# SwiGLU's gate and up products with the weights stationary instead of the activations

## The chip, the cores and the metric

The kernel runs on one core of one Trainium2 chip. The metric is device time of that core in microseconds (us). The kernel before took 2026.13 us, the median of three runs (2023.01, 2026.13, 2027.49).

## What is computed

Two stacks of two layers each over 256 tokens of width 1024, all in float32:

```
first stack, twice:   x = x + 0.5 * swiglu(rms_norm(x, g0))
                      x = x + mixer(rms_norm(x))         # two attentions in layer 0, latent attention in layer 1
                      x = x + memory_attention(rms_norm(x), rms_norm(mem))
                      x = x + 0.5 * swiglu(rms_norm(x, g1))
second stack, twice:  x = layer_norm(alpha * x + mixer2(x))
                      x = layer_norm(alpha * x + swiglu(x))
swiglu(h) = (silu(h @ w_gate) * (h @ w_up)) @ w_down     # 1024 -> 2816 -> 1024
rms_norm(x, gain) = x * rsqrt(mean(x * x) + 1e-6) * gain
```

There are six SwiGLUs, each with three weights of 2,883,584 numbers.

## The kernel before

**Dense products.** The 256 tokens are cut into two halves of 128. Float32 operands are split into two parts of type float32r, hi and lo, and a product is the sum in PSUM of three: lo x hi, hi x lo, hi x hi. Weights come in tiles of 512 KB (128 partitions x 1024 numbers): `weights` (L137 to L151) loads one by a DMA on SyncE's queue into one of four kept `wr` slots (L132), ScalarE writes its hi part `wh` (L149, three kept slots), VectorE the lo part `wl` (L150, two kept slots).

**`dense` (L187 to L211)** has the activations stationary: for each half and each block of 128 rows of the weight it issues

```
nc.tensor.matmul(o, xl, wh[:, k], start=first, stop=False)    # L207
nc.tensor.matmul(o, xh, wl[:, k], start=False, stop=False)    # L208
nc.tensor.matmul(o, xh, wh[:, k], start=False, stop=last)     # L209
```

where `xh`, `xl` are 128 features x 128 tokens (tiles `op`, `ol`), and up to 512 columns of the weight move past them. The result has tokens on the partitions. One PSUM bank per half takes it. The last tiles can be held apart (`apart`), in the scope's own `wh` and `wl` slots, to be used for half 0 first.

**`swiglu` (L290 to L311)** takes 512 of the 2816 features at a time (five blocks, and one of 256): the gate product, ScalarE's SiLU straight from PSUM with the norm's r as scale (L303), the up product, VectorE's multiplication of both (L306), and `split_T` (L214 to L225): TensorE transposes the four blocks of each half (L221), ScalarE writes their hi part (L224), VectorE the lo part (L225). Then the down product runs over all 22 blocks, 512 result columns at a time, in 11 tiles each; for the second 512 columns the last four tiles are held apart.

**Around it.** `norm_T` (L261 to L286) makes the transposed operand of the normed x: blocks 0 to 3 of both halves, then blocks 4 to 7. Its rms factor r per token is left to who takes the products (`xT.r`). `ffn1` (L313 to L322) adds half the result to x. `ffn2` (L985) has no norm in front; behind it `post` and `ln` (L943 to L983) do the layer norm, half by half. `dense_T` (L991 to L1013), used in `mixer2`, has the weights stationary and both halves' 256 tokens moving; its matmuls go through `Chain` (L416 to L428; the matmul is L423), which keeps the products into one bank in program order.

**Order of the work and place of the tiles.** Each engine runs its own queue in order; the compiler's scheduler sets the order by program order, with what `later` moves and dependencies. The slots of a phase are given in `SCOPES` by tag; sizes by tag are in `SIZES`: `s` and `ls` slots have 16 float32 columns (64 bytes per partition), all others 128 columns or multiples. A phase's pools lie one behind the other in SBUF in the order of that table, after the kept tiles.

Of the kernel before, what the change touches and what calls it, by code (L numbers as in the profile page):

```python
"""Two stacks of two layers on one core: diff / stick-breaking / latent / memory attention and
SwiGLU with pre-norm, then gated linear attention, RWKV-7 and sparse attention with post-norm.

Dense products: the operands are split exactly into two float32r parts (12 and 11 significant bits)
and three products of parts are summed in PSUM, which keeps float32's accuracy. Tokens are cut into
two halves of 128; the halves' chains are independent but for keys and values."""
# [22 lines left out]
class Core:  # L29
    """Pools, the splitting of float32 operands and the dense products."""  # L30

    # columns of a tile by tag
    SIZES = (("s", 16), ("b05", 128), ("b1", 256), ("b2", 512), ("b4", 1024), ("b8", 2048))
    # slots by phase and tag: in SBUF and in PSUM
    KEEP = dict(x=2, g1=4, v1=1, wr=4, wh=3, wl=2)
    SCOPES = {
        "ffn": (dict(s=10, ls=14, g4=2, b2=6, op=8, ol=8, wh=4, wl=4),
                dict(t=2, d=6)),
        "ffn2": (dict(s=10, ls=8, b2=8, op=8, ol=8, wh=4, wl=4, g2=4),
# [27 lines left out]
    @contextmanager  # L67
    def scope(self, name):
        """Pools of a phase."""
        self.n += 1  # L70
        self.caps = self.SCOPES[name]
        self.count = {}
        self.turn = -1
        with ExitStack() as st:
            pool = lambda t, **k: st.enter_context(self.tc.tile_pool(name=f"{name}_{t}_{self.n}", bufs=1, reuse_waits="tile", **k))
            self.sb = {t: pool(t) for t in self.caps[0] if t != "chains"}
            self.ps = {t: pool(t + "p", space=PSUM) for t, n in self.caps[1].items() if not isinstance(n, str)}
            yield
# [35 lines left out]
    def evac(self, out, in_, scale=None):  # L114
        """PSUM to SBUF, by ScalarE and VectorE in turn."""
# [9 lines left out]
    def raw_weights(self, parts, k0, nk):  # L125
        """Rows k0 : k0 + nk * 128 of parts [(w, first column, columns)] side by side, as [128, nk, columns]."""
# [8 lines left out]

    def weights(self, parts, k0, nk, room=None):
        """The same as (hi, lo), in the kept tiles or in those of the tags in room: one for each, or one for both."""  # L137
        nc = self.nc
        raw = self.raw_weights(parts, k0, nk)
        n = raw.shape[2]  # L140
# [28 lines left out]
    def on(self, stream):  # L169
        """Slots of its own for what the block traces."""  # L170
# [4 lines left out]
    def chain(self):  # L175
        """One of the streams C0, C1, ... in turn: their work overlaps."""
# [4 lines left out]
    def later(self, n):  # L181
        """What the block traces is issued as if traced n instructions later."""
# [4 lines left out]
    def dense(self, lhs, w, n0, nw, done, order=None, apart=()):  # L187
        """Token-major product of 512 columns at most: lhs(h, k) gives the (hi, lo) of the kth block of
        128 rows of the transposed operand of half h; done(h, psum) takes the result. The last tiles of the
        weights, held as apart says one by one, are all used for the first half before the second."""  # L190
# [23 lines left out]
    def split_T(self, src, nb, put):  # L214
        """src [128 tokens, nb blocks of 128] to the (hi, lo) views put(b, m)."""
# [12 lines left out]
    def rstd(self, ss, n, mean_scale, eps, r=None):  # L228
        """(ss * mean_scale + eps) ** -0.5 of [128, n]."""
# [7 lines left out]
    def row_gain(self, ap, n):  # L237
        """A vector on every partition."""
# [5 lines left out]
    def operand(self, nb, groups=None):  # L244
        """Room for nb transposed blocks of both halves, in groups of four or [(tag, blocks)]: put(h, b, m) gives
        the (hi, lo) views [128, m, 128] of blocks b : b + m (within a group), get(h, k) the (hi, lo) of one."""
# [6 lines left out]
        get.both = lambda k: [v[at[k][0]][:, at[k][1]] for v in V]  # L253
        return put, get

    def twin(self):
        """Two long-lived tiles of 256 columns."""
# [3 lines left out]
    def norm_T(self, xs, gain, gates=True):  # L261
        """The transposed and split halves, a function (h, k) -> (hi, lo). With a gain: of the product by it,
        and r[h], what the rms norm multiplies the rows of half h by, is left to who takes the products."""
# [5 lines left out]
        for i in range(2):  # L269
            # the first half may run ahead of the product that still works on the second  # L270
# [19 lines left out]
    def swiglu(self, xT, wg, wu, wd, done):  # L290
        """done(h, n0, psum): columns n0 : n0 + 512 of half h."""
        nc = self.nc
        F = wg.shape[1]
        r = getattr(xT, "r", (1.0, 1.0))
        put, get = self.operand(F // 128)

        for n0 in range(0, F, 512):
            nw = min(512, F - n0)
            g = {}

            def gate(h, ps):
                g[h] = self.t(512)
                nc.scalar.activation(g[h][:, :nw], ps, AF.Silu, scale=r[h])  # L303

            def up(h, ps):
                nc.vector.scalar_tensor_tensor(g[h][:, :nw], ps, r[h], g[h][:, :nw], op0=OP.mult, op1=OP.mult)  # L306
                self.split_T(g[h], nw // 128, lambda b, m: put(h, n0 // 128 + b, m))

            self.dense(xT, wg, n0, nw, gate)
            self.dense(xT, wu, n0, nw, up)  # L310
# [3 lines left out]
    def ffn1(self, layer, j):  # L314
        nc, I = self.nc, self.I
        gain = self.row_gain(I["ffn_norm"][layer, j], 1024)
        xT = self.norm_T(self.x, gain)

        def done(h, n0, ps):
            x = self.x[h][:, n0:n0 + 512]  # L320
            nc.vector.scalar_tensor_tensor(x, ps, 0.5, x, op0=OP.mult, op1=OP.add)

        self.swiglu(xT, I["ffn_w_gate"][layer, j], I["ffn_w_up"][layer, j], I["ffn_w_down"][layer, j], done)

# [1 line left out]
    def load_consts(self, cp):  # L326
        """The constants that the first phase needs."""
# [4 lines left out]
        self.mhalf = self.c["mhalf"]  # L332

    def load_masks(self, cp, cb):
        """The others."""
# [20 lines left out]
def const_pack():  # L356
    """Constants that depend on shapes alone: those in float32, and masks that bfloat16 holds exactly."""
# [4 lines left out]
    # -1 where the row's key is not before the column's, and everywhere  # L362
# [12 lines left out]
    # even tokens, then odd ones  # L375
# [9 lines left out]
    b["causal"] = np.where(c > p, -1e30, 0.0)       # queries on partitions  # L385
    b["strict"] = np.where(p >= c, -1e30, 0.0)      # keys on partitions
    b["keep64"] = np.broadcast_to(np.arange(256)[None] % 64 != 0, (128, 256))
    # within chunks of 64 rows
# [22 lines left out]
# of them: those that the first phase needs  # L411
# [4 lines left out]
class Chain:  # L416
    """Products into one PSUM bank, kept in this order on the tensor engine."""
# [13 lines left out]
class Mix1(Core):  # L431
# [10 lines left out]
    def head_rstd(self, src, nh, d, eps=1e-6, times=1.0, r=None):  # L442
        """times / rms over the d columns of each head of [128, nh * d] (a view [128, nh, d])."""
# [8 lines left out]
    def to_T(self, src, nb, out, w=128, scale=None):  # L452
        """src [128 tokens, nb * w] to out (view [w, nb, 128], or several of rows [(rows, view)])."""
# [18 lines left out]
    def rope_into(self, out, x, nh, d, cos, sin):  # L472
        """out = rotated x, both views [128, nh, d]; cos [128, d] and sin [128, d] carry the gains."""
# [10 lines left out]
    def rope_gain(self, room, cs, sn, gain, d, scale=1.0):  # L484
        """Tables of [128, d] with a gain [128, d] folded in."""
# [1348 lines left out]
```

## Time and profile before

| | |
|---|---|
| median of three runs | 2026.13 us |
| span of the profiled execution | 2021.1 us |
| mean granted clock of TensorE in it | 0.992 |
| busy: TensorE, weight loads, VectorE, ScalarE, GpSimd | 97%, 80%, 60%, 49%, 9% |
| DMA: bytes moved, mean rate | 318.76 MB, 158 GB/s |

The profile is of one execution. Its page gives the span, from the first instruction to the last, and no other time of that execution; 5.0 us separate it from the median of the runs. Times in the rows count from the start of the span. PE is TensorE's matmuls, PEld its weight loads, DVE VectorE, ACT ScalarE, POOL GpSimd, SP SyncE. Matmuls overlap, so the duration of one is longer than the distance between two starts.

### The profile page before, as it was taken

How to read it: one execution, taken by the hardware profiler on the slowest of the kernel's cores; microseconds unless marked ns; L12 is line 12 of the kernel's file. 1: busy time of each engine (PE TensorE's matmuls, PEld its weight loads, DVE VectorE, ACT ScalarE, POOL GpSimd, SP SyncE). 2: the span in 40 equal slices, each digit the busy share in tenths (PEclk: the TensorE clock that was granted, in tenths of full speed). 3: DMA queues.
4: the chain of work that ended last, by engine and by line, in shares of the span. 5: the costliest groups of instructions: out<-in, count | busy, mean ns of one | idle time of the engine just before them, and what ended most of it. 6: DMA issues, size and time to landing. Idle time of an engine off the chain costs nothing.

```text
span 2021.1 us, 28782 instructions
## 1 busy us (share of the span) xinstructions
PE 1951.2 (97%) x10916; PEld 1613.1 (80%) x10916; DVE 1220.9 (60%) x1849; ACT 990.4 (49%) x1549; POOL 191.2 (9%) x269
## 2 busy tenths in 40 slices
PE   8999999899999999898999999999999999999998
PEld 6888778788878888677888888777888787777886
DVE  5555765655555557766655567666555667565555
ACT  5444556554444446655544445543444455434442
POOL 0000401000000001330000012310000213210000
PEclk9999999999999999999999999999999999999999
DMA  7666543466556656234566654314666644026654
GB/s 226 188 194 223 152 136 106 125 198 186 184 179 188 185 193 210 89 100 146 167 187 179 210 148 125 106 43 144 180 180 184 180 140 155 2 84 188 185 179 136
DMA packets 198556, 318.76 MB, mean 158 GB/s; under 512 B 28944, under 2 KB 61969, under 8 KB 198417
## 3 DMA queue, kind: packets, MB, share of 16 engines
q1 hardware_dynamic: 197824, 315.79, 52.2%
q8 instruction: 86, 1.41, 0.3%
q0 software_dynamic: 160, 0.52, 0.1%
q10 hardware_dynamic: 432, 0.60, 0.1%
q14 instruction: 54, 0.43, 0.1%
HBM read 315.82 MB, written 1.05 MB: 157 GB/s over the span
## 4 chain that ended last, share of the span: by engine, by line
PE 53%; DVE 3%; ACT 1%; issue 1%; DMA 1%; POOL 0%; SPq 0%; DVEq 0%; ACTq 0%; POOLq 0%
PE pd L207 12%; PE pd L208 12%; PE pd L209 12%; PE pd L423 4%; PE po L423 2%; PE ppC L423 1%; DVE wl L150 1%; PE pt L221 1%; PE pg L1190 1%; PE pg L423 1%; PE pt L459 0%; PE pq L1466 0%; PE pq L1475 0%; PE pq L700 0%; DMA wr<-in_w_in_dram 0%
## 5 line engine op out<-in xcount | busy, mean ns | idle before, releaser
L150 DVE TENSOR_TENSOR wl<-wr,wh 128x1024 fp32r<-128x1024 f32 (+2 forms) x557 | 677.7, 1219 | 517.0 <-PE pd L208 391.6
L149 ACT ACTIVATE wh<-wr 128x1024 fp32r<-128x1024 f32 (+2 forms) x557 | 585.0, 1051 | 604.0 <-PE pd L209 511.3
L208 PE MATMUL pd<-wl,op 128*128 128x512 f32 (+4 forms) x2136 | 810.1, 380 | 3.9 <-DVE wl L150 3.8
L209 PE MATMUL pd<-wh,op 128*128 128x512 f32 (+4 forms) x2136 | 805.2, 378 | 0.0
L207 PE MATMUL pd<-wh,ol 128*128 128x512 f32 (+4 forms) x2136 | 749.5, 380 | 8.3 <-DVE ol L225 6.9
L207 PEld LDWEIGHTS pd<-wh,ol 128*128 128x128 f32 x2136 | 401.3, 189 | 83.5 <-DVE ol L225 8.4
L208 PEld LDWEIGHTS pd<-wl,op 128*128 128x128 f32 x2136 | 403.6, 189 | 79.4 <-DVE wl L150 7.3
L209 PEld LDWEIGHTS pd<-wh,op 128*128 128x128 f32 x2136 | 403.8, 189 | 71.7
L224 ACT ACTIVATE op<-pt 128x512 fp32r<-128x512 f32 (+1 forms) x118 | 65.8, 564 | 82.6 <-PE pt L221 82.6
L225 DVE TENSOR_TENSOR ol<-pt,op 128x512 fp32r<-128x512 f32 (+1 forms) x118 | 77.0, 656 | 31.7 <-ACT op L224 31.2
L234 POOL TENSOR_TENSOR ls<-s,cf 128x1 f32<-128x1 f32 (+2 forms) x30 | 25.5, 851 | 743.7 <-DVE s L233 563.4
L221 PE MATMUL pt<-cf,b 128*128 128x128 f32 x404 | 63.4, 279 | 11.3 <-DVE b L276 7.9
L221 PEld LDWEIGHTS pt<-cf,b 128*128 128x128 f32 x404 | 50.8, 143 | 24.2 <-DVE b L276 8.3
L423 PE MATMUL pd<-op,wl 128*128 128x256 f32 x208 | 58.5, 281 | 6.3 <-DVE lb2R L1266 4.8
L234 POOL TENSOR_TENSOR s<-s,cf 128x1 f32<-128x1 f32 (+2 forms) x22 | 22.7, 1032 | 442.4 <-DVE s L233 441.1
L423 PE MATMUL pd<-ol,wh 128*128 128x256 f32 x208 | 58.1, 279 | 0.0
L423 PE MATMUL pd<-op,wh 128*128 128x256 f32 x208 | 57.8, 278 | 0.0
L423 PEld LDWEIGHTS pd<-op,wl 128*128 128x128 f32 x208 | 39.1, 188 | 7.5 <-DVE lb2R L1266 5.4
L306 DVE SCALAR_TENSOR_TENSOR b<-pd,ls,b 128x512 f32<-128x512 f32 (+1 forms) x48 | 33.8, 703 | 12.6 <-PE pd L209 12.6
L303 ACT ACTIVATE b<-pd,ls 128x512 f32<-128x512 f32 (+1 forms) x48 | 31.3, 654 | 20.2 <-PE pd L209 20.1
L423 PEld LDWEIGHTS pd<-ol,wh 128*128 128x128 f32 x208 | 39.1, 188 | 0.8 <-issue 0.7
L423 PEld LDWEIGHTS pd<-op,wh 128*128 128x128 f32 x208 | 39.1, 188 | 0.7 <-issue 0.7
(496 smaller groups left out, 1981.2 us busy)
## 6 DMA issues: line engine op xcount, KB each, us to landing
wr<-in_ffn_w_gate_dram SPq DMA_DIRECT2D x132, 512.0 KB, 3.7
wr<-in_ffn_w_up_dram SPq DMA_DIRECT2D x132, 512.0 KB, 3.7
wr<-in_ffn_w_down_dram SPq DMA_DIRECT2D x132, 512.0 KB, 3.7
wr<-in_w_in_dram SPq DMA_DIRECT2D x45, 512.0 KB, 4.6
wr<-in_ab_w_in_dram SPq DMA_DIRECT2D x24, 512.0 KB, 4.2
wr<-in_xm_w_kv_dram SPq DMA_DIRECT2D x16, 512.0 KB, 3.7
wr<-in_w_out_dram SPq DMA_DIRECT2D x16, 512.0 KB, 4.2
wr<-in_ab_w_out_dram SPq DMA_DIRECT2D x8, 512.0 KB, 3.6
```

The costliest lines, as they stand in the source:

```text
L149: nc.scalar.activation(hi, raw, AF.Copy)
L150: nc.vector.tensor_tensor(lo, raw, hi.bitcast(F32), op=OP.subtract)
L207: nc.tensor.matmul(o, xl, wh[:, k], start=first, stop=False)
L208: nc.tensor.matmul(o, xh, wl[:, k], start=False, stop=False)
L209: nc.tensor.matmul(o, xh, wh[:, k], start=False, stop=last)
L221: nc.tensor.transpose(pt[:, i * 128:(i + 1) * 128], src[:, (b0 + i) * 128:(b0 + i + 1) * 128], self.ident)
L224: nc.scalar.activation(hi, v, AF.Copy)
L225: nc.vector.tensor_tensor(lo, v, hi.bitcast(F32), op=OP.subtract)
L234: self.pow = nc.gpsimd.tensor_tensor(r, a, self.mhalf[:, :n], op=OP.pow)
L303: nc.scalar.activation(g[h][:, :nw], ps, AF.Silu, scale=r[h])
L306: nc.vector.scalar_tensor_tensor(g[h][:, :nw], ps, r[h], g[h][:, :nw], op0=OP.mult, op1=OP.mult)
L423: i = self.k.nc.tensor.matmul(out, lhsT, rhs, start=start, stop=stop, skip_group_check=skip)
```

## The change

The gate and up weights are repacked on the host into one array, `ffn_gu` (and `ffn_gu_2`): 11 groups of 256 features, four quarters of the 1024 rows each, and for a group and quarter one contiguous piece of 128 x 1024 numbers that holds, for two blocks of 128 rows, 128 gate columns, 128 up columns, 128 gate columns, 128 up columns. `packed` loads such a piece by one DMA; the splitting (`parted`) stays as it was.

`swiglu` walks over groups. A group has two PSUM banks, each with 256 columns (all tokens) of a gate block and 256 of an up block, and per tile 4 x 2 x 3 matmuls in which 128 x 128 of the weight is stationary and the 256 tokens of both halves move. The result has features on the partitions, as the down product wants its operand, so `split_T` isn't called. Since r now lies along the row, `along` builds a matrix R with r of each token on all partitions, by two plain float32 matmuls (ones x diagonal of r) behind the first group's products; VectorE multiplies the gate by R ahead of SiLU. The up product's r is applied to the result of the down product, as 0.5 r. In `ffn2` there is no r, and SiLU reads PSUM. The down product's code is unchanged. `SCOPES` gets the slots for this.

```diff
-        "ffn": (dict(s=10, ls=14, g4=2, b2=6, op=8, ol=8, wh=4, wl=4),
+        "ffn": (dict(s=10, ls=16, g4=2, b2=6, b1=6, b05=2, lb1=1, op=8, ol=8, wh=4, wl=4),
                 dict(t=2, d=6)),
-        "ffn2": (dict(s=10, ls=8, b2=8, op=8, ol=8, wh=4, wl=4, g2=4),
+        "ffn2": (dict(s=10, ls=8, b2=6, b1=6, op=8, ol=8, wh=4, wl=4, g2=4),
                 dict(t=3, d=5)),
...
+    def packed(self, w, nk):
+        raw = self.kept("wr", 1024)
+        self.nc.sync.dma_start(raw, w)
+        return self.parted(raw.rearrange("p (k n) -> p k n", k=nk))
...
+        get.blocks = lambda b, m: [v[at[b][0]][:, at[b][1]:at[b][1] + m] for v in V]
...
-    def swiglu(self, xT, wg, wu, wd, done):
-        nc = self.nc
-        F = wg.shape[1]
-        r = getattr(xT, "r", (1.0, 1.0))
-        put, get = self.operand(F // 128)
-        for n0 in range(0, F, 512):
-            nw = min(512, F - n0)
-            g = {}
-            def gate(h, ps):
-                g[h] = self.t(512)
-                nc.scalar.activation(g[h][:, :nw], ps, AF.Silu, scale=r[h])
-            def up(h, ps):
-                nc.vector.scalar_tensor_tensor(g[h][:, :nw], ps, r[h], g[h][:, :nw], op0=OP.mult, op1=OP.mult)
-                self.split_T(g[h], nw // 128, lambda b, m: put(h, n0 // 128 + b, m))
-            self.dense(xT, wg, n0, nw, gate)
-            self.dense(xT, wu, n0, nw, up)
+    def along(self, r):
+        nc = self.nc
+        pt, R = self.p("t"), self.l(256)
+        for h in range(2):
+            d = self.t(128)
+            nc.vector.tensor_scalar(d, self.ident, r[h], None, op0=OP.mult)
+            nc.tensor.matmul(pt[:, h * 128:(h + 1) * 128], self.ones, d, start=True, stop=True)
+        nc.scalar.activation(R, pt[:, :256], AF.Copy)
+        return R
+
+    def swiglu(self, xT, wgu, wd, done):
+        nc = self.nc
+        G = wgu.shape[0]
+        put, get = self.operand(2 * G)
+        R = None
+        for g in range(G):
+            banks = [self.p("d") for _ in range(2)]
+            chains = [Chain(self) for _ in banks]
+            for q in range(4):
+                wh, wl = self.packed(wgu[g, q], 2)
+                for i in range(4):
+                    o = banks[i // 2][:, (i % 2) * 256:(i % 2) * 256 + 256]
+                    ch = chains[i // 2]
+                    c = slice(i * 128, i * 128 + 128)
+                    for k in range(2):
+                        xh, xl = xT.both(2 * q + k)
+                        first, last = q == 0 and k == 0, q == 3 and k == 1
+                        ch(o, wl[:, k, c], xh, start=first and i % 2 == 0, stop=False, skip=True)
+                        ch(o, wh[:, k, c], xl, start=False, stop=False, skip=True)
+                        ch(o, wh[:, k, c], xh, start=False, stop=last, skip=True)
+            if R is None and hasattr(xT, "r"):
+                R = self.along(xT.r)
+            y = self.t(512)
+            for b, ps in enumerate(banks):
+                s = self.t(256)
+                if R is None:
+                    nc.scalar.activation(s, ps[:, :256], AF.Silu)
+                else:
+                    nc.vector.tensor_tensor(s, ps[:, :256], R, op=OP.mult)
+                    nc.scalar.activation(s, s, AF.Silu)
+                nc.vector.tensor_tensor(y[:, b * 256:b * 256 + 256], ps[:, 256:], s, op=OP.mult)
+            yv = y.rearrange("p (b t) -> p b t", b=2)
+            hi, lo = get.blocks(2 * g, 2)
+            nc.scalar.activation(hi, yv, AF.Copy)
+            nc.vector.tensor_tensor(lo, yv, hi.bitcast(F32), op=OP.subtract)
         for n0 in range(0, 1024, 512):
             self.dense(get, wd, n0, 512, lambda h, ps: done(h, n0, ps), apart=[("wh", "wl")] * 4 if n0 else ())
...
+        half = [self.l(1) for _ in range(2)]
+        for h in range(2):
+            nc.vector.tensor_scalar(half[h], xT.r[h], 0.5, None, op0=OP.mult)
         def done(h, n0, ps):
             x = self.x[h][:, n0:n0 + 512]
-            nc.vector.scalar_tensor_tensor(x, ps, 0.5, x, op0=OP.mult, op1=OP.add)
+            nc.vector.scalar_tensor_tensor(x, ps, half[h], x, op0=OP.mult, op1=OP.add)
...
+        self.ones = self.consts.tile([128, 128], F32, name="ones")
+        self.nc.gpsimd.memset(self.ones, 1.0)
```

## Rows read from the trace of the kernel before

**Rows 1.** The page, busy us, share of the span, instructions by engine.
```profile
PE 1951.2 (97%) x10916; PEld 1613.1 (80%) x10916; DVE 1220.9 (60%) x1849; ACT 990.4 (49%) x1549; POOL 191.2 (9%) x269
```
**Rows 2.** The page, chain that ended last, share of the span by line.
```profile
PE pd L207 12%; PE pd L208 12%; PE pd L209 12%; PE pd L423 4%; PE po L423 2%; PE ppC L423 1%; DVE wl L150 1%; PE pt L221 1%; PE pg L1190 1%; PE pg L423 1%; PE pt L459 0%; PE pq L1466 0%; PE pq L1475 0%; PE pq L700 0%; DMA wr<-in_w_in_dram 0%
```
**Rows 3.** Windows: us; busy PE, PEld, DVE, ACT, POOL; clock, DMA, GB/s.
```profile
404.10:529.75 125.65, 125.65 (x624) 106.00 (x622) 70.67 (x73) 61.42 (x72) 1.12 (x2) 1.00 0.64 189
529.75:590.89 61.14, 61.14 (x278) 50.45 (x276) 33.36 (x34) 28.00 (x33) 0.55 (x1) 1.00 0.64 206
...
1396.67:1521.36 124.69, 124.69 (x604) 103.59 (x605) 67.20 (x66) 58.32 (x67) 0.00 (x0) 1.00 0.61 178
```
**Rows 4.** Timeline of PE, `ffn1`, 512 columns: start, duration, line, tiles, shape, count.
```profile
110.43 0.63 PE L207 MATMUL pd<-wh,ol 128*128 128x512 f32 x2
...
126.57 0.39 PE L209 MATMUL pd<-wh,op 128*128 128x512 f32 x1
```
**Rows 5.** Timeline of PE, `ffn1`, the last block of 256 columns.
```profile
131.61 0.28 PE L209 MATMUL pd<-wh,op 128*128 128x256 f32 x1
...
139.05 0.28 PE L209 MATMUL pd<-wh,op 128*128 128x256 f32 x1
```
**Rows 6.** Timeline of PE, `ffn2`, 512 columns.
```profile
1446.01 0.62 PE L207 MATMUL pd<-wh,ol 128*128 128x512 f32 x2
...
1465.53 0.63 PE L207 MATMUL pd<-wh,ol 128*128 128x512 f32 x2
```
**Rows 7.** Timeline of PE, `ffn2`, the last block of 256 columns.
```profile
1513.78 0.28 PE L208 MATMUL pd<-wl,op 128*128 128x256 f32 x1
...
1521.25 0.28 PE L209 MATMUL pd<-wh,op 128*128 128x256 f32 x1
```
**Rows 8.** Timeline of PE, `dense_T` in the two layers of `mixer2`.
```profile
1188.25 0.28 PE L423 MATMUL pd<-ol,wh 128*128 128x256 f32 x1
...
1198.94 0.28 PE L423 MATMUL pd<-op,wh 128*128 128x256 f32 x1
...
1599.76 0.28 PE L423 MATMUL pd<-op,wl 128*128 128x256 f32 x1
...
1605.06 0.28 PE L423 MATMUL pd<-op,wl 128*128 128x256 f32 x1
```
**Rows 9.** Timeline of PE around four transposes of a result in `ffn1`.
```profile
38.64 0.62 PE L207 MATMUL pd<-wh,ol 128*128 128x512 f32 x2
39.10 0.60 PE L221 MATMUL pt<-cf,b 128*128 128x128 f32 x4
...
39.77 0.39 PE L209 MATMUL pd<-wh,op 128*128 128x512 f32 x1
```
**Rows 10.** Timeline of PE, start of the first `ffn2`; in brackets idle before, releaser.
```profile
1390.21 0.51 PE L207 MATMUL pd<-wh,ol 128*128 128x512 f32 x1 [2.07 <-DVE ol L225]
...
1396.67 0.50 PE L207 MATMUL pd<-wh,ol 128*128 128x512 f32 x1 [0.54 <-DVE ol L225]
```
**Rows 11.** Windows of PE: us, busy, granted clock, DMA, GB/s; both `ffn2` starts.
```profile
1391.20:1394.60 3.40, 3.40 (x9) 0.52 1.02 332
...
1822.00:1826.00 4.00, 4.00 (x24) 1.00 0.97 307
```
**Rows 12.** Timeline of all engines, start of the second and of the third `ffn1`.
```profile
405.28 1.28 DVE L225 TENSOR_TENSOR ol<-pt,op 128x512 fp32r<-128x512 f32 x2
...
592.75 0.63 PE L221 MATMUL pt<-cf,b 128*128 128x128 f32 x4 [1.47 <-DVE ol L225]
```
**Rows 13.** The page, costliest groups: busy, mean ns, then idle before, releaser.
```profile
L150 DVE TENSOR_TENSOR wl<-wr,wh 128x1024 fp32r<-128x1024 f32 (+2 forms) x557 | 677.7, 1219 | 517.0 <-PE pd L208 391.6
L149 ACT ACTIVATE wh<-wr 128x1024 fp32r<-128x1024 f32 (+2 forms) x557 | 585.0, 1051 | 604.0 <-PE pd L209 511.3
L208 PE MATMUL pd<-wl,op 128*128 128x512 f32 (+4 forms) x2136 | 810.1, 380 | 3.9 <-DVE wl L150 3.8
```
**Rows 14.** The page, DMA issues: count, KB each, median us from issue to landing.
```profile
wr<-in_ffn_w_gate_dram SPq DMA_DIRECT2D x132, 512.0 KB, 3.7
```

More of the change, by code (lines that the diff above doesn't have):

```diff
@@ L134, in raw_weights, with parted @@
         return v
+    def packed(self, w, nk):
+        raw = self.kept("wr", 1024)
+        self.nc.sync.dma_start(raw, w)
+        return self.parted(raw.rearrange("p (k n) -> p k n", k=nk))
     def weights(self, parts, k0, nk, room=None):
+        return self.parted(self.raw_weights(parts, k0, nk), room)
+    def parted(self, raw, room=None):
         nc = self.nc
-        raw = self.raw_weights(parts, k0, nk)
-        n = raw.shape[2]
+        nk, n = raw.shape[1:]
         if room is None:
@@ L317, in ffn1 @@
         xT = self.norm_T(self.x, gain)
+        half = [self.l(1) for _ in range(2)]
+        for h in range(2):
+            nc.vector.tensor_scalar(half[h], xT.r[h], 0.5, None, op0=OP.mult)
         def done(h, n0, ps):
             x = self.x[h][:, n0:n0 + 512]
-            nc.vector.scalar_tensor_tensor(x, ps, 0.5, x, op0=OP.mult, op1=OP.add)
-        self.swiglu(xT, I["ffn_w_gate"][layer, j], I["ffn_w_up"][layer, j], I["ffn_w_down"][layer, j], done)
+            nc.vector.scalar_tensor_tensor(x, ps, half[h], x, op0=OP.mult, op1=OP.add)
+        self.swiglu(xT, I["ffn_gu"][layer, j], I["ffn_w_down"][layer, j], done)
     def load_consts(self, cp):
@@ L987, in ffn2 @@
         self.post("ln2", layer, "g2", lambda done: self.swiglu(
-            xT, I["ffn_w_gate_2"][layer], I["ffn_w_up_2"][layer], I["ffn_w_down_2"][layer], done))
+            xT, I["ffn_gu_2"][layer], I["ffn_w_down_2"][layer], done))
     def dense_T(self, both, parts, done):
@@ L1793 @@
 _INS = [
-    "x", "mem", "ffn_norm", "ffn_w_gate", "ffn_w_up", "ffn_w_down", "mix_norm", "ab_w_in", "ab_w_out",
+    "x", "mem", "ffn_norm", "ffn_w_down", "mix_norm", "ab_w_in", "ab_w_out",
     "diff_q_norm", "diff_k_norm", "diff_lambda_q1", "diff_lambda_k1", "diff_lambda_q2", "diff_lambda_k2",
@@ L1801, with gate_up @@
     "nsa_pos_v_2", "nsa_wk1_2", "nsa_wk2_2", "nsa_wv1_2", "nsa_wv2_2", "w_out_2", "ln1_w_2", "ln1_b_2",
-    "ffn_w_gate_2", "ffn_w_up_2", "ffn_w_down_2", "ln2_w_2", "ln2_b_2",
+    "ffn_w_down_2", "ln2_w_2", "ln2_b_2",
 ]
+def gate_up(g, u):
+    both = np.stack([np.asarray(w).reshape(*w.shape[:-2], 4, 2, 128, w.shape[-1] // 256, 2, 128) for w in (g, u)], -2)
+    n = both.ndim - 7
+    both = both.transpose(*range(n), n + 3, n, n + 2, n + 1, n + 4, n + 5, n + 6)
+    return np.ascontiguousarray(both).reshape(*both.shape[:n + 3], 1024)
 def kernel(**inputs):
@@ L1821 @@
         add(name, _np.ascontiguousarray(inputs[name]))
+    add("ffn_gu", gate_up(inputs["ffn_w_gate"], inputs["ffn_w_up"]))
+    add("ffn_gu_2", gate_up(inputs["ffn_w_gate_2"], inputs["ffn_w_up_2"]))
     add("constants", CONST)
```

## Prediction

> **What bounds the kernel now.** I read the page's busy shares first: TensorE is busy 97% of the span, and neither VectorE (60%) nor ScalarE (49%) comes near it [rows 1]. The chain of work that ended last says the same from the other end: three lines, the three products of `dense`, hold 36% of the span between them, and no other line over 4% [rows 2]. So the next question is not who waits but how long one step of TensorE's stream is. The windows view answers for the changed stage: a SwiGLU's gate and up part takes 125.65 us in an `ffn1`, with TensorE busy for all of it; its down part 61.14, likewise; in `ffn2` the gate and up part is 124.69 us from the first product of the second half on [rows 3]. A stage without idle time is priced by counting instructions and reading their start-to-start step off the timeline.
>
> **The step, by form.** Matmuls overlap, so I take two starts in an undisturbed run and divide by the steps between. In `ffn1`, 512 columns moving: 71 steps from 110.43 to 126.57, 227.3 ns [rows 4]. The last 256 features of an `ffn1`, 256 columns moving: 62 steps from 131.61 to 139.05, 120.0 ns [rows 5]. In `ffn2` the same two forms differ: 84 steps from 1446.01 to 1465.53, 232.4 ns [rows 6], and 63 steps from 1513.78 to 1521.25, 118.6 ns [rows 7]. The form that the change brings (weights stationary, 256 tokens moving) runs already in `dense_T`: 94 steps from 1188.25 to 1198.94, 113.7 ns; but the same line, 45 steps from 1599.76 to 1605.06, took 117.8 [rows 8]. So a 256-column step costs anything from 113.7 to 120.0 ns in these rows; two of them make 227 to 240 where one 512-column step makes 227 to 232. The change turns 480 of the latter and 96 of the former into 1056 of the former. That is the whole question.
>
> What goes with these steps in the code is where the pools put the operands. Tiles are laid one behind the other in SBUF and all but the small `s` and `ls` slots (64 bytes) are multiples of 512 bytes. With 10 + 14 such slots in `ffn`, `op` stands 1536 bytes, a multiple of 256, behind the kept `wh`: 227.3 and 120.0. With 10 in `ffn2` (its `ls` is unused) the distance leaves 128: 232.4 and 118.6. With 11 in `m2` it leaves 192, which is 64 taken the other way round, as `dense_T` does: 113.7. This is a pattern of these rows, not a proof, and the 117.8 run breaks it. The change makes `ls` 16, so `ffn` gets 1664 bytes, which leaves 128 like `ffn2`. So in all six SwiGLUs the gate and up stream should have the distance of [rows 7]: I take 118.6 ns, between the ends 113.7 and 120.0.
>
> **Part by part**, against the profiled execution, whose span is 2021.1 us; the median of the three runs is 2026.13, so 5.0 us lie around the span and are added at the end.
>
> 1. *Transposes of the results.* 44 per SwiGLU go. From 38.64 to 39.77 stand three 512-column matmuls and four transposes in 1.13 us [rows 9]; three steps of 0.227 leave 0.45 us for the four. Ten such groups lie inside the 125.65 us: 480 x 0.2273 + 96 x 0.1200 + 10 x 0.45 = 125.1, so that sum explains the stage but for 0.5 us. The eleventh group stands among the first down products and goes from there: 6 x -0.45 = -2.7 us.
> 2. *Gate and up of the four `ffn1`.* 1056 x 0.1186 = 125.24 us, plus the matrix R: two plain float32 products of 128 columns, which I price like the four transposes, 0.45 (0 to 1). 125.7 against 125.65: 4 x 0.04 = +0.2 us. What ten groups of transposes give, the longer step takes back.
> 3. *Down of the four `ffn1`.* The code is the same, but `op` has moved. 216 of its 264 matmuls take weights from the kept tiles and get `ffn2`'s distance; the 48 of the four tiles held apart lie behind `op` in the same scope and keep theirs. 216 x (232.4 - 227.3) = +1.10 us each, +4.4 for four (0 to 5).
> 4. *Gate and up of the two `ffn2`.* Now the first matmul needs both halves. Before, twelve matmuls of half 0 ran from 1390.21 in the shade of the second half's layer norm; half 1 was transposed behind them and its first product started at 1396.67, having waited 0.54 us for VectorE [rows 10]. Those twelve are no longer hidden: from 1396.67 on there are all 1056, 125.24 instead of 124.69: +0.55. From 1390.21 to 1396.67 TensorE then has only the second half's transposes, some 6 us of near idleness. After an idle of 2.07 us the granted clock was 0.52 (the lower level, 1.2 GHz) from 1391.20 to 1394.60, 3.40 us for some eight steps, 0.43 each instead of 0.23; in the second `ffn2` the same place had 1.00 [rows 11]. Before, that lay in the shade; now it is on the path: 8 x 0.2 = +1.6 (0 to 1.7). Behind the waiting matmul stand only its own stream and the weights' tiles. With TensorE free, the second half's transposes may also go earlier: 0 to -1. Together +2.15 each, +4.3 for two (-1 to +5).
> 5. *Starts of the `ffn1`.* The second started at 404.10 [rows 3] on half 0, while VectorE wrote two `ol` of the other groups from 405.28 to 406.56; the first matmul now waits for one of them, to about 405.9, +1.8, and the fourth in the same way. Between the second and the third, 1.47 us of idle waited for `ol` [rows 12]; the first tile needs two blocks of both halves only, so some 1.2 to 1.5 of it may go. The first SwiGLU waits for its input as before. Sum +2 us (-1.5 to +4).
> 6. *Evacuation.* Per 256 features now: four `wl` at 1.22, four products of 128x256 and one of 128x512 on VectorE. I bound each of the five by 0.64, the 128x512 write of `ol` [rows 12]: 4.9 + 3.2 = 8.1 of the 11.4 us that 96 steps take. ScalarE: four `wh` at 1.05 and three smaller ones at 0.53 to 1.05, under 7.4 [rows 13]. Hidden under TensorE: 0; its price without cover is rival C.
> 7. *One piece per tile.* The same 512 KB per transfer and as many of them; 4 KB rows instead of 2. A tile landed 3.7 us after its issue [rows 14], four `wr` slots deep, and one is used up in 24 x 0.1186 = 2.85 us; the transfers are hidden already, no product waits for one in [rows 3]. 0 us, either way. The constants, `half` and the 128x128 of ones: off the path, 0.
>
> Sum: -2.7 + 0.2 + 4.4 + 4.3 + 2 = +8.2 us. Span 2029, time 2029.3 + 5.0 = 2034 us.
>
> The lowest 256-column step of these rows is 113.7 ns, in `dense_T` [rows 8]. The Trainium skill, "TensorE: Matmul & The Clock Gate", section "Back-to-back issue gap", gives N / 2.4 + 2.5 ns for the isolated gap, 109.2 ns at 256 columns, and lets the weight load weigh in as well; by its gap alone the 1056 would take an estimated 115.3 us, some 60 us less over six stages. The rows don't come down to it, and its figure for 512 columns, 215.8, stands under every step of [rows 4, 6], so the rows decide.
>
> **Rivals.**
> A. *The step of `dense_T`.* Same instruction form, same order of the three products, 113.7 ns: the nearest row by form, where my choice is the nearest by placement. 6 x 1056 x -4.9 ns = -31.0 us: 2003 us, faster. It decides as soon as the step is under 117.3 ns (8.2 / 6336 = 1.3 ns under mine). Against it: the two forms at distance 128 agree with each other and neither shows 113.7. Shorter steps than that would be in here too; for them I see one chance in fifty.
> B. *The step of `ffn1`'s own last block*, 120.0: +1.4 x 6336 = +8.9 us, 2043. For it: it is the row of the same weights in the same stage; against it: the distance changes.
> C. *Evacuation delays the weights.* VectorE's queue is in order; a group's end is a product by R, a wait for ScalarE's SiLU, a second product, a wait for the copy, a subtraction. Placed in one piece that is some 3.3 us ahead of the next `wl`, and with two `wl` slots there is 2.85 - 1.22 = 1.6 us to spare. It costs nothing while the pieces are spread between the `wl`, and begins to count when over 1.6 us of them stand together. If 0.3 us per group shows: 66 x 0.3 = +20 us, 2054. Against it: before, pairs of 0.7 us stood there too, and L208 waited for `wl` under 4 us in the whole span [rows 13].
> D. *A mixture of steps.* One line stands at 113.7 and at 117.8 with the same distance of its operands [rows 8], so something else can shift the step too. Half of the groups at 113.7 and half at 118.6, 116.15 on average: 6336 x -2.45 ns = -15.5 us, 2019.
>
> **Chances.** Forecast 48%, A 22%, B 10%, C 10%, D 10%. The forecast's own range is 2027 to 2042. 0.2%, 4 us, is what a measurement can tell from no change, that is 2022 to 2030. Faster: A 22 and most of D, 30%. Same: the low end of the forecast, the rest of D, 15%. Slower 55%. The range of 8 in 10 is 2000 to 2046: most of A lies inside, B too, C mostly outside.
>
> **What would show it.** In the profile after: steps of the stationary-weights lines read off the timeline, 118.6 in both `ffn` and `ffn2` (113.7: A; 120: B; a change within a stage: D); gate and up stages of 125.7 us; the down stage of `ffn1` at 62.2 instead of 61.1; an idle of 6 us or more before each `ffn2` with a granted clock near 0.5 behind it. Idle time of the products for `wl` or for PSUM of over 10 us shows C. If gate and up stages come out near 120 us, the choice of the step was wrong and with it the sign.

## The result and the profile after

The changed kernel took 2046.6 us (median of 4 runs, 2043.56 to 2048.2), the kernel before 2024.57 us on the same chip: 1.011 times as long, 95% interval 1.0095 to 1.0126. Slower, as forecast, but by 22 us where 8 were forecast, and just above the range. The profiled span is 2046.5 us, 25.4 us over that of before.

TensorE's busy time hardly moved (1951.2 us in [rows 1]); the span grew by four times as much:

```profile
PE 1957.1 (96%) x13548; PEld 1740.0 (85%) x13548; DVE 1257.9 (61%) x2007; ACT 1007.6 (49%) x1607; POOL 190.9 (9%) x270
```

So some 20 us are idle time. The windows of the changed kernel say where. Below stand the first two SwiGLUs and the stretches behind the first and the third, then an `ffn2` (columns as in [rows 3]; first product to first down product, then down):

```profile
14.15:142.50 128.35, 128.35 (x1061) 128.35 (x1062) 77.31 (x102) 63.26 (x79) 0.36 (x1) 1.00 0.60 184
203.34:414.50 211.16, 195.02 (x1018) 157.72 (x1017) 139.07 (x235) 118.00 (x204) 36.18 (x33) 0.97 0.42 130
414.50:542.85 128.35, 128.05 (x1067) 127.85 (x1066) 77.91 (x107) 63.38 (x80) 1.12 (x2) 0.99 0.60 184
542.85:604.62 61.77, 61.77 (x274) 50.30 (x272) 33.84 (x35) 28.34 (x33) 0.55 (x1) 1.00 0.61 203
795.92:998.18 202.26, 178.84 (x987) 143.17 (x985) 142.43 (x298) 120.01 (x256) 38.94 (x60) 0.97 0.39 120
1420.80:1548.40 127.60, 127.60 (x1058) 127.60 (x1057) 68.27 (x77) 60.90 (x77) 0.00 (x0) 0.99 0.57 174
```

The same two stretches behind the first and the third SwiGLU in the kernel before, from the last down product to the next gate product:

```profile
200.27:404.10 203.83, 193.73 (x1011) 156.51 (x1009) 134.53 (x226) 116.32 (x201) 33.38 (x32) 0.97 0.43 131
779.67:974.47 194.80, 177.94 (x983) 142.12 (x981) 138.64 (x291) 118.09 (x253) 41.53 (x59) 0.98 0.39 117
```

These hold the mixers and the memory attention, whose code the change doesn't touch. They grew by 7.33 and 7.46 us, of which only 1.3 and 0.9 are busy time of TensorE. That is 14.8 of the 25.4 us. The rest, stage by stage: gate and up of the four `ffn1` +1.92, +2.70, +3.29, +0.98 (8.9), their down products -0.27, +0.63, +1.24, +0.64 (2.2), the lead to the first SwiGLU +1.4 and to the third -2.0; of the second stack the stretches ahead of the two `ffn2` (counted to half 1's first product before, to the first product after) -1.2 and -1.6, their gate and up +2.9 and +1.3, down -0.65 each. Sum 25.4.

**Inside the stages the forecast step stood.** The second SwiGLU, from the second group's first product to the last one, 959 steps:

```profile
428.93 0.28 PE L467 MATMUL pd<-op,wl 128*128 128x256 f32 x1
...
542.73 0.28 PE L467 MATMUL pd<-op,wh 128*128 128x256 f32 x1
```

113.80 us through 959 is 118.7 ns, and a group of 256 features, 96 products, is 11.39 us in five of the six stages (forecast: 118.6 ns a product). In the first `ffn2` it is 11.52, 120.0 ns. But the first groups are longer: 14.42, 14.42, 15.02, 12.72, 12.40 and 11.99 us. The first SwiGLU shows what is in them, 22 steps from 14.53 to 19.22, 213 ns each:

```profile
14.53 0.41 PE L467 MATMUL pd<-ol,wh 128*128 128x256 f32 x1
...
19.22 0.41 PE L467 MATMUL pd<-op,wh 128*128 128x256 f32 x1
```

213 ns for 256 columns is a column per cycle at 1.2 GHz. In the first SwiGLU the clock's column reads 1.00 all the same; but the first record of the clock in this trace stands at 19.7 us, and a stretch ahead of it reads 1.00 for want of a record, so that the clock was at its lower level there is inferred from the step alone. In the second the granted clock itself says so (us, busy, clock, DMA, GB/s):

```profile
415.70:418.90 3.20, 3.20 (x17) 0.50 0.73 274
418.90:422.00 3.10, 3.10 (x28) 0.97 0.10 25
```

**Where the mixers' time went.** The waits of the changed kernel's TensorE (203 to 414 us), and of VectorE (203 to 215 us): TensorE waited 5.5 us for the product of x by the norm gain, and VectorE for the gain's transfer.

```profile
PE pt L229 <- DVE b L285: 5.5, 1, 5.5
```

```profile
DVE b L285 <- DMA g<-in_mix_norm_dram: 3.9, 1, 3.9
```

SyncE's queue shows when that transfer was issued: before, at 141.10 us, between the first SwiGLU's down weights; after, at 204.58, behind the last update of x. First the kernel before, then the changed one, with the update (L363; its operand `ls` is `half`) and what the queue waited for:

```profile
141.10 0.81 SPq L163 DMA_DIRECT2D g<-in_mix_norm_dram  x2
```

```profile
197.59 6.51 SPq L798 DMA_DIRECT2D lb<-in_mem_dram  x2
203.77 0.75 DVE L363 SCALAR_TENSOR_TENSOR x<-pd,ls,x 128x512 f32<-128x512 f32 x1 [4.69 <-PE pd L217]
204.58 0.80 SPq L171 DMA_DIRECT2D g<-in_mix_norm_dram  x2
```

```profile
SPq L171 <- DVE x L363: 0.4, 1, 0.4
```

### The profile page after: what moved, and what is told of

Its sections match the earlier page's. It is cut to its first block, busy times and chain, and to the rows that moved or that the text cites. A ratio compares the mean times of both kernels' runs of the same rounds, so it can differ in the third digit from the quotient of the medians.

```text
span 2046.5 us, 34153 instructions
## 1 busy us (share of the span) xinstructions
PE 1957.1 (96%) x13548; PEld 1740.0 (85%) x13548; DVE 1257.9 (61%) x2007; ACT 1007.6 (49%) x1607; POOL 190.9 (9%) x270
## 4 chain that ended last, share of the span: by engine, by line
PE 53%; DVE 3%; ACT 1%; issue 1%; DMA 1%; POOL 0%; SPq 0%; DVEq 0%; ACTq 0%; POOLq 0%
PE pd L467 23%; PE pd L216 6%; PE pd L215 6%; PE pd L217 6%; PE po L467 2%; DVE wl L158 1%; PE ppC L467 1%; PE pg L1234 1%; PE pg L467 1%; PE pr L1510 0%; PE pt L503 0%; PE pq L1510 0%; PE pq L1519 0%; PE pt L229 0%; PE pq L1515 0%
## 5 line engine op out<-in xcount | busy, mean ns | idle before, releaser
L467 PE MATMUL pd<-op,wl 128*128 128x256 f32 x2320 | 656.2, 283 | 8.3 <-DVE lb2R L1310 4.5
L467 PE MATMUL pd<-ol,wh 128*128 128x256 f32 x2320 | 656.1, 283 | 0.4 <-DVE ol L233 0.3
L467 PE MATMUL pd<-op,wh 128*128 128x256 f32 x2320 | 653.9, 282 | 0.0
L467 PEld LDWEIGHTS pd<-op,wl 128*128 128x128 f32 x2320 | 438.7, 189 | 10.4 <-DVE lb2R L1310 5.0
L467 PEld LDWEIGHTS pd<-ol,wh 128*128 128x128 f32 x2320 | 439.4, 189 | 1.6 <-DVE ol L233 0.8
L467 PEld LDWEIGHTS pd<-op,wh 128*128 128x128 f32 x2320 | 439.7, 190 | 0.7 <-issue 0.7
L216 PE MATMUL pd<-wl,op 128*128 128x512 f32 (+5 forms) x984 | 378.5, 385 | 4.3 <-DVE wl L158 4.1
L217 PE MATMUL pd<-wh,op 128*128 128x512 f32 (+5 forms) x984 | 375.3, 382 | 0.0
L215 PE MATMUL pd<-wh,ol 128*128 128x512 f32 (+5 forms) x984 | 357.7, 386 | 2.8 <-DVE ol L233 1.7
L216 PEld LDWEIGHTS pd<-wl,op 128*128 128x128 f32 x984 | 186.4, 189 | 41.4 <-DVE wl L158 6.6
L217 PEld LDWEIGHTS pd<-wh,op 128*128 128x128 f32 x984 | 186.4, 189 | 35.3
```

The source lines that it names most:

```text
L467: i = self.k.nc.tensor.matmul(out, lhsT, rhs, start=start, stop=stop, skip_group_check=skip)
```

## The experiments

**S (the slots) or Q (the order of the products): why was the gain late?** A phase's pools lie where the last phase's were. The gain slot of `m0` and `m1` begins 1152 bytes behind the kept tiles (8 `s` and 10 `ls` slots of 64), and the `ls` slots of `ffn` reach from 640 to 1664. If the change takes two of the topmost for `half`, which the very last instruction on x reads, whoever writes a gain over them has to wait for it. No view prints the addresses, so this is a theory. The first experiment shortens the `ls` pool so that `half` lies below, whichever slots it takes.

```diff
-        "ffn": (dict(s=10, ls=16, g4=2, ...
+        "ffn": (dict(s=10, ls=4, g4=2, ...
```

> The changed kernel with 4 instead of 16 `ls` slots in `ffn`, and nothing else. Theory S (slots): the changed kernel lost 7.3 and 7.5 us between the end of the first and third SwiGLU and the next product, because the new `half` tiles lie where the next phase puts its norm gain, so that the gain's load waits for the last update of x. With 4 slots `half` lies below that place. Byte distance of `op` to the kept weights stays at 128 (mod 256). S expects those two stretches back at 204 and 195 us and the time 14.8 us under the changed kernel's, about 2032; every gate and up step stays at 118.6 ns. Rival Q: the load is late because the products ahead of it are now issued in another order, whatever the slots: the time stays at 2046.

Measured: 2031.31 us, 1.0048 times the kernel before (1.0031 to 1.0065; before 2022.2 in these runs). The two stretches are back:

```profile
202.36:404.52 202.16, 190.01 (x1015) 153.59 (x1013) 136.62 (x230) 117.37 (x203) 35.19 (x32) 1.00 0.44 134
785.10:980.61 195.51, 177.33 (x983) 141.62 (x981) 140.07 (x295) 119.73 (x255) 39.71 (x60) 0.98 0.39 121
```

and the gain is issued early again:

```profile
145.53 0.42 SPq L171 DMA_DIRECT2D g<-in_mix_norm_dram  x1
```

All groups but the first stay at 11.39 us. Q falls: no product was reordered. The other direction, the slots alone put into the kernel before:

```diff
+        half = [self.l(1) for _ in range(2)]
+        for h in range(2):
+            nc.vector.memset(half[h], 0.5)
...
-            nc.vector.scalar_tensor_tensor(x, ps, 0.5, x, op0=OP.mult, op1=OP.add)
+            nc.vector.scalar_tensor_tensor(x, ps, half[h], x, op0=OP.mult, op1=OP.add)
```

> The kernel before, with one thing of the change: the 0.5 of `ffn1`'s last step (L321) comes from two `ls` tiles filled with 0.5, taken behind the norm as `half` is in the changed kernel. No product, weight layout or step is touched. Theory S: these tiles lie where `m0` and `m1` put their norm gain, its load waits for the last update of x, and the two stretches behind the first and the third SwiGLU grow by 7 to 8 us each: 2037. Rival Q (the loss came with the new order of the products): 2022, as the kernel before.

Measured: 2034.12, 1.0056 times the kernel before (1.0035 to 1.0077; before 2023.87). The two stretches took 210.00 and 202.37 us instead of 203.83 and 194.80, and its TensorE (198 to 420 us) shows the wait of the changed kernel:

```profile
PE pt L221 <- DVE b L276: 5.6, 1, 5.6
```

S is shown from both sides. The other runs agree: the first of these loads was issued at 141 to 149 us in the traces with 4, 5 and 7 `ls` slots, and at 198 to 205 in all four that have `half` and 14 slots or more. Two tiles of one column cost the old kernel 10 us, less than the 15 expected and than the 13.7 by which the two stretches grew.

**D (the distance of the two operands) or E (what the other engines do): what sets the step?** Three placements, nothing else changed: 17 slots and 18 (`ffn2` moved alike), and 16 in the kernel before. The first as a diff:

```diff
-        "ffn": (dict(s=10, ls=16, ...        "ffn2": (dict(s=10, ls=8, ...
+        "ffn": (dict(s=10, ls=17, ...        "ffn2": (dict(s=11, ls=8, ...
```

> The changed kernel with 17 instead of 16 `ls` slots in `ffn` and 11 instead of 10 `s` slots in `ffn2`: `op` and `ol` move by 64 bytes, `half` stays where the next phase's gain goes. Theory D (distance): the step of a 256-column product follows the distance of its two operands mod 256, and the new one is that of `dense_T`. D expects 113.7 ns per step instead of 118.6 in all six gate and up stages, groups of 10.9 instead of 11.39 us, 31 us in all, about 2015 us; the down steps at 229 to 232 ns, within 1 us per stage of what they were. Rival E (engines): the step is set by what VectorE, ScalarE and the DMA do beside it, which stays as it was: 118.6 and 2046.

Measured: 2030.28 in the median of ten runs, 1.0028 times before (1.0004 to 1.0053), where 2015 was expected, and spread from 2014.82 to 2035.12, while the run with 4 slots kept within 2 us. In its trace each stage settles on one of two steps and keeps it to its end. In the profiled run four stages had groups of 10.88 us and the third and fourth 11.31. The second stage, 240 steps (113.3 ns), and the third, 240 steps (117.8 ns), of the same kernel in the same execution:

```profile
500.87 0.28 PE L467 MATMUL pd<-op,wh 128*128 128x256 f32 x1
...
528.07 0.28 PE L467 MATMUL pd<-op,wh 128*128 128x256 f32 x1
...
690.46 0.28 PE L467 MATMUL pd<-op,wh 128*128 128x256 f32 x1
...
718.72 0.28 PE L467 MATMUL pd<-op,wh 128*128 128x256 f32 x1
```

So D is right on what is to be had and half right on what comes: at distance 64 both steps exist, and these are the two of [rows 8]. Which one comes was settled in the few steps behind an interruption (transposes, the products for R, idle time): in the second stage the step was 113.3, then 117.8 behind four transposes, then 113.3 behind the products for R.

> As the run with 17 and 11 slots, with 18 and 12: distance 0. D expects 120.0 ns in all gate and up stages (groups of 11.52 us, 1.5 us more per stage than the changed kernel) and 227.2 in the down products (1.1 us less per stage), so about the changed kernel's time, within 4 us. E expects 118.6.

Measured: 2045.84 (one run). All groups behind the first are 11.52 us, 120.0 ns, in all six stages; down stages took 59.64 to 61.18 instead of 60.84 to 62.13 us. As D said.

> The kernel before with 16 instead of 14 `ls` slots in `ffn`, and nothing else: its four `ffn1` get the distance 128 of its `ffn2`. D expects their 512-column steps at 232.4 instead of 227.3 ns, those of 256 columns at 118.6 instead of 120.0, so gate and up 125.65 + 480 x 5.1 - 96 x 1.4 ns = 128.0 us, down 62.2 instead of 61.1, in all 4 x 3.4 = 13.8 us more than before: about 2038. E expects no change: 2024.

Measured: 2039.03, 1.0084 times the kernel before (1.0055 to 1.0114). Two slots that nothing uses cost some 17 us. In the profiled execution, 19.3 us longer than that of the kernel before, 13.3 us stand in the eight stages of the four `ffn1` (13.8 were expected) and 6.1 in the mixer behind the third, which the edit doesn't touch; there the granted clock was 0.94 instead of 0.98. Gate and up, and down, of its second SwiGLU, where [rows 3] have 125.65 and 61.14:

```profile
406.60:534.45 127.85, 127.85 (x623) 106.27 (x621) 70.67 (x73) 61.37 (x72) 1.11 (x2) 1.00 0.63 185
534.45:596.78 62.33, 62.33 (x278) 50.53 (x276) 33.45 (x34) 28.02 (x33) 0.55 (x1) 1.00 0.61 202
```

128.0 and 62.2 were expected; VectorE, ScalarE and the transfers do the same work. E falls.

All these edits move `op` and `ol` and leave the kept weights where they are, so the address of `op` alone could still be what counts. The changed kernel's own down products decide that. Their first 216 take kept weights, at distance 128; the last 48 take the four tiles held apart, which lie behind `op` in the same scope, at distance 0, while `op` stays where it is. The first of its down stages, 167 steps and then 45:

```profile
153.64 0.40 PE L215 MATMUL pd<-wh,ol 128*128 128x512 f32 x1
...
192.45 0.40 PE L217 MATMUL pd<-wh,op 128*128 128x512 f32 x1
193.14 0.39 PE L217 MATMUL pd<-wh,op 128*128 128x512 f32 x1
...
203.34 0.39 PE L217 MATMUL pd<-wh,op 128*128 128x512 f32 x1
```

That is 232.4 and 226.7 ns in one stream; in the run with 18 slots, where both are at distance 0, it is 226.7 ns in the same stage from end to end. So neither operand's address alone sets the step. Distances that differ by 768 bytes (4 and 16 slots, 5 and 17) give the same steps, as D has it. Two looks at more distances:

> The run with 4 `ls` slots, with 7 of them, and one slot of 32 bytes in `ffn2`: a look at two more distances, 192 in the four `ffn1` and 96 in the two `ffn2` (stationary less moving operand, mod 256). D expects 117.8 ns per step at 192, which the 256-column products of `mixer2` have with activations stationary; for 96 it has no row: between 113.3 and 118.6. E expects 118.6 at both.

> The run with 4 `ls` slots, shifted by slots of 32 and 64 bytes to two more distances of stationary and moving operand in gate and up: 32 in the four `ffn1` and 224 in the two `ffn2`. D says that the step follows the distance: between 113.3 (64) and 120.0 (0) for 32, between 117.8 (192) and 120.0 (0) for 224. E expects 118.6 at both.

Measured (one run each, 2030.54 and 2025.74): at 192 all four stages 11.31 us (117.8 ns); at 96 11.26 in one stage and 11.39 in the other; at 32 all four 11.36 (118.3); at 224 both 11.20 (116.7). The 116.7 lies under the 117.8 to 120.0 expected for 224, so the steps between two measured distances can't be read off their neighbours. The step of a 256-column product went 120.0, 118.3, 113.3 or 117.8, 117.3 or 118.6, 118.6 (once 120.0), 117.8, 116.7 for distances 0, 32, 64, 96, 128, 192, 224 bytes. The Trainium skill, "TensorE: Matmul & The Clock Gate", section "Step-by-step: what each phase is for", says that TensorE reads its two operands by two ports and that loading the next weights takes nothing from the running product. These steps, which hang on where the one operand lies to the other, speak against reading that as "placement doesn't matter"; what in the chip does it no run here shows.

**C (the clock) or M (the transfers and evacuations beside them): the slow first steps.** On top of the 4 `ls` slots, extra products ahead of the first one, to keep TensorE at work:

```diff
...
                 wh, wl = self.packed(wgu[g, q], 2)
+                if g == q == 0:
+                    warm = self.p("d")
+                    for _ in range(12 if hasattr(xT, "r") else 40):
+                        nc.tensor.matmul(warm[:, :128], wh[:, 0, :128], xT(0, 0)[0], start=True, stop=True)
```

> The run with 4 `ls` slots, and on top of it products whose result nobody reads, ahead of each SwiGLU's first product: 12 (`ffn1`) or 40 (`ffn2`) of 128 columns on half 0's operand, into a PSUM bank of their own. Theory C (clock): the first products of a stage took 213 ns instead of 118.6 because TensorE, which now waits for both halves, had idled and was granted 1.2 GHz. In the run with 4 slots the first groups of 96 products were 12.83, 14.45, 14.97, 12.70, 12.24 and 11.84 us; less 11.39, the products for R, transposes and idle time among them, about 1.0, 1.9, 0.6, 0.3, 0.9 and 0.5 us of each are such steps, 5.1 us. C expects most of them to go, 3 to 5 us, 2027. Rival M: the slow steps come from the first transfers and evacuations that run beside them; they stay, and the extra products only add: 2031 to 2035.

Measured: 2037.08, 1.0068 times before (1.0052 to 1.0083): 6 us above the run with 4 slots in the median, though the two intervals overlap. 2027 was expected by C.

C is borne out in the first `ffn2`. The 8 us ahead of its first product and the 1.6 behind it, with 4 slots and then with the extra products (us, busy, clock, DMA, GB/s):

```profile
1395.81:1403.81 8.00, 2.93 (x18) 0.68 0.80 260
1403.81:1405.41 1.60, 1.60 (x9) 0.50 0.00 0
1401.42:1409.42 8.00, 6.81 (x60) 1.00 0.80 260
1409.42:1411.02 1.60, 1.38 (x11) 1.00 0.03 10
```

In all nine traces of the changed kernel and its variants without extra products the clock stood at 0.50 at or just ahead of this start; here it doesn't, and the six steps of 213 ns that the run with 4 slots has behind its first product are gone. In the second `ffn2` the clock fell all the same, but early, during the extra products:

```profile
1833.12:1841.12 8.00, 8.00 (x46) 0.59 0.53 188
```

In the second SwiGLU the slow steps are gone, too, right from the first product:

```profile
409.10 1.53 PE L327 MATMUL pd<-op,wh 128*128 128x128 f32 x12
410.48 0.45 PE L471 MATMUL pd<-op,wl 128*128 128x256 f32 x2
410.76 0.28 PE L471 MATMUL pd<-ol,wh 128*128 128x256 f32 x1
410.88 0.28 PE L471 MATMUL pd<-op,wh 128*128 128x256 f32 x1
```

But there it proves nothing: six of the nine traces without extra products have full speed at this start as well, behind the same wait, and the other three 18 or 19 slow steps. The run with two weight arrays below, as an example:

```profile
407.65:410.85 3.20, 2.90 (x25) 1.00 0.80 255
```

So whether this stage meets the lower clock changes from execution to execution, and one trace of a run can't show what removed it. In the first SwiGLU the extra products themselves came at steps of 213 ns, where in the second the same ones came at 108 to 115, and the slow steps went on behind them. M falls where the clock itself reads 0.50 over the slow steps; why the clock falls at one start and not at another is open.

As for the price: the first groups of the last five stages came to 4.4 us less than with 4 slots (2.1 of it in the second, where chance has a part, and 1.3 in the third, which lost idle time and no slow steps). But the extra products stand in the same queue, and the stretches ahead of the first four stages grew by 2.6, 2.0, 1.3 and 3.4 us. Filling the wait brought no gain here.

**P (off the path) or L (late tiles): the layout alone.** With 4 `ls` slots, the weights in two arrays again:

```diff
...
-                wh, wl = self.packed(wgu[g, q], 2)
+                wh, wl = self.weights([(wg, g * 256, 256), (wu, g * 256, 256)], q * 256, 2)
...
```

> The run with 4 `ls` slots, but with the gate and up weights as they were, in two arrays: each tile of 512 KB comes by two transfers with rows of 1 KB instead of one with rows of 4 KB; products and their order stay. Theory P: the layout is off the path, since a tile is used for 2.85 us and four are in flight: gate and up groups stay at 11.39 us, time 2031, within 4 us. Rival L: the shorter rows and twice the transfers on SyncE's queue bring tiles late; products wait for `wl`, groups grow to 12 us or more, 6 x 11 x 0.6 = 40 us more.

Measured: 2032.02, 1.0059 times before (1.0037 to 1.0082), against 1.0048 (1.0031 to 1.0065) with the pieces: no difference that can be told. Groups stay at 11.39 us.

**Both findings together.**

```diff
-        "ffn": (dict(s=10, ls=16, ...        "ffn2": (dict(s=10, ls=8, ...
+        "ffn": (dict(s=10, ls=5, ...         "ffn2": (dict(s=11, ls=8, ...
```

> The changed kernel with 5 `ls` slots in `ffn` and 11 `s` slots in `ffn2`: `half` clear of the next phase's gain (S) and distance 64 everywhere (D). The two edits add up if they are independent: the run with 17 and 11 slots had 2030 in the median of 10 (2015 to 2035) with each stage at 113.3 or 117.8 ns; less 14.8 that is 2015 in the median, between 2000 and 2020, and so under the kernel before, by 0 to 1%. If the slots were not the cause, 2030.

Measured: 2010.01, 0.9935 times the kernel before (0.9921 to 0.9949): with two numbers changed, the change is a gain. In the profiled run two stages took the short step and four the long one:

```profile
406.14:527.51 121.37, 121.08 (x1067) 120.87 (x1066) 77.78 (x107) 62.85 (x80) 1.12 (x2) 1.00 0.64 193
588.80:716.56 127.76, 126.16 (x1070) 125.50 (x1069) 79.14 (x107) 62.04 (x79) 0.55 (x1) 1.00 0.57 174
```

Last, x's operand and the down operand at distances of their own (`opX`, `olX` behind 11 `s` slots at the end of the scope, the down operand at 0):

> The changed kernel with two placements in the SwiGLUs: the normed x's operand in slots of its own at distance 64 from the kept weights, the down product's operand at distance 0, `half` clear of the next phase's gain. By D gate and up stages step at 113.3 or 117.8 ns as in the run with 5 and 11 slots (2010), and the down stages at 227.2 instead of 229 to 232 (59.7 us instead of 60.2 to 61.4), 0.5 to 1.5 us less each, 3 to 9 in all: 2001 to 2007, mid 2005. If the down steps don't follow the distance, 2010.

Measured: 2014.62, 0.9962 times before (0.9948 to 0.9976): under the kernel before, but above the 2001 to 2007 expected and above the run with 5 and 11 slots. The down stages did fall, to 59.61 to 60.59 us, but in the profiled run the mixer behind the third SwiGLU took 203.7 us where the run before it took 193.2, at a granted clock of 0.85 to 0.88 for 100 us of it (there 1.00) and with nearly the same waits. Why the clock was lower is open. The run with 5 and 11 slots remains the best.

## Why the prediction was wrong

*The step that failed* is the last sentence of step 7: "The constants, `half` and the 128x128 of ones: off the path, 0." I asked what `half` costs to make, not what lies at its address in the next phase. It cost 14.8 us in the profiled run, and taking its slots away brings the time to 1.0048 times before; 8.2 us of 2026, the forecast, is 1.0040. The gain's load stood in SyncE's queue at 141.10 us of the trace before, and nothing in that trace said that it could go so early only because those slots were idle; the run of the kernel before with the two tiles alone showed it.

*Steps 1 and 3*, transposes and down: forecast -2.7 and +4.4, together +1.7. Measured +2.2 in the down stages of the four `ffn1` and -1.3 in the two `ffn2`, +0.9. Right within a microsecond, and the split into 216 and 48 down products is in the trace (232.4 and 226.7 ns). The 62.2 us named as a sign for the down stage left out the -0.45 of step 1; the sum's own figure is 61.8, and the four measured 60.84, 61.77, 62.13 and 60.90.

*Step 2*, gate and up at 118.6 ns: right to a tenth of a nanosecond for 10 of 11 groups in five stages, in the choice by placement against the nearer form, and E's fall shows that placement was the reason. Rival B's 120.0 ns came in one stage, the first `ffn2`, at the same distance, and cost 1.3 us there. *Steps 2 and 5 together* were mis-sized at the starts: +2.2 forecast, +8.3 measured in gate and up and the two leads. I priced the cold clock for `ffn2` alone, because the trace before showed it there [rows 11]; but every stage now waits for both halves, and in this execution 15 and more steps of 213 ns stand in each of the first two `ffn1`. How many come differs from trace to trace: in the other eight without extra products the first SwiGLU has 9 to 23; the second has 18 or 19 in two of them and at most four in six, which would be 1.5 us less. So part of the 8.3 is chance. The third's +3.3 is partly the lead's -2.0, transposes and idle time that now lie behind the first product. *Step 4*: +4.3 forecast, +1.4 measured; the cold steps were there (7 and 3 of them), but with the twelve products of half 0 gone from the queue the second half was ready 1.2 and 1.6 us earlier. So it is in part luck that all but the slots came to 10.6 us (25.4 less 14.8) where 8.2 were forecast: steps 2 and 5 were 6.1 too low, step 4 was 2.9 too high.

*Step 6*: no wait for `wl` grew (rival C of the prediction didn't come). In the whole span the products of gate and up (with the others of L467) waited 0.6 us for it and the products of L216 4.1, where those of L208 had waited 3.8 before [rows 13]:

```profile
PE pd L216 <- DVE wl L158: 4.1, 7, 1.4
PE pd L467 <- DVE wl L158: 0.6, 1, 0.6
```

*Step 7*'s first half, the layout, was right: 0.

Rival A, the step of `dense_T`, was no rival but a choice: 64 bytes more would have brought it, in some of the stages. The 109.2 ns that come, as an estimate, of the isolated gap at 256 columns in the Trainium skill's "TensorE: Matmul & The Clock Gate", section "Back-to-back issue gap", were reached by no stream of such products in any trace here: 113.3 was the least.

## What to carry to other kernels

When a change adds a long-lived tile, however small, look up which tile of the next phase gets its address and when that one is first written: a load may lose its head start. Price a stream of matmuls by a row with the same distance between stationary and moving operand, and before moving a tuned loop try two or three paddings: here 64 bytes in each SwiGLU took the run with 4 slots from 2031 to 2010 us. A product that needs all of its input at once has an idle TensorE ahead of it; give its first steps a range from full speed to the lower clock, which was worth some 2 us per stage here and differed between executions.

## What was not expected of the hardware

The step of a stream of matmuls followed the distance of its two operands modulo 256 bytes: 113.3 to 120.0 ns with 256 columns moving, and 226.7 to 232.4 with 512, both ends of the latter in one stage of one execution.

At one distance two steps can exist: 113.3 and 117.8 ns at 64 bytes, and likewise 117.3 and 118.6 at 96, 118.6 and 120.0 at 128. A stream keeps the one that it has behind its last interruption to the end of its stage, over 960 products. All six stages on one step of the first pair instead of the other would make 6 x 960 x 4.5 ns = 26 us, room enough for the 20 us by which the run with 17 and 11 slots spread (2014.82 to 2035.12). Only one of its ten executions was traced, so that this made the spread is not shown; the kernel before spread over 11 us, too.
